# Projections of an attention block: granules of 512 instead of 256 moving columns, in four PSUM banks

## The chip, the core and the metric

The kernel runs on one core of a Trainium2 chip. The metric is the device time of one launch in microseconds (us). A core has a matrix engine (TensorE, PE in the profile, with its weight loads as PEld), a vector engine (VectorE, DVE), a scalar engine (ScalarE, ACT), GpSimd (POOL) and SyncE (SP), which here issues nearly all DMA transfers. Each engine works through its own queue in order and waits on semaphores for the others. TensorE multiplies a stationary 128x128 tile with moving columns and writes to PSUM, of which this kernel uses eight banks of 128 partitions x 512 float32.

## The reference

One decoder layer: RMSNorm of x (512 tokens, 1024 channels), one input projection whose columns are split among a state-space branch, an attention branch and gates, then two output projections, a gated sum, a last projection `w_o` and the residual. What matters here, cut:

```python
h = rms_norm(x, norm_w[layer])
proj = h @ w_in[layer]
u_s, z_s, q, k, v, z_a, r_s, r_a = jnp.split(proj, offsets, axis=-1)
y_s = s5_branch(u_s, ...)                       # diagonal state space, GELU, GLU
y_s = (y_s * silu(z_s)) @ w_ssm_out[layer]
q = apply_partial_rope(rms_norm(q.reshape(B, L, 3, 8, 64), q_norm_w), positions)
k = apply_partial_rope(rms_norm(k.reshape(B, L, 3, 8, 64), k_norm_w), positions)
y_a = dilated_attention(q, k, v.reshape(B, L, 3, 8, 64))   # 3 head groups, 8 heads of 64
y_a = (y_a * silu(z_a)) @ w_attn_out[layer]
m = sigmoid(r_s) * y_s + sigmoid(r_a) * y_a
x = x + m @ w_o[layer]
```

All arithmetic is float32.

## The kernel before, in words

**Matmuls in three parts.** To multiply float32 values at the faster rate of the type fp32r, each operand is split into a high and a low part (`split`, lines 90 to 97: ACT rounds to the high part, DVE or POOL subtracts). One product is then three matmuls, `mm3` (lines 107 to 110): high x high, high x low, low x high. The normed input is kept transposed and split as `hT_hi`, `hT_lo` (1024 channels in 8 slices of 128, 512 tokens).

**Weights** come in the order of a list, `plan`. Each entry is a tile of 128 x 1024 values, 512 KB: `cm_spec` takes 128 columns over all 8 slices of the contraction; `tok_spec` takes 256 columns in two tiles, each of 4 slices (a half of the contraction). `load_w` lets SP issue a DMA for every separate run of columns (line 166), then splits the tile on ACT (line 93, `w_hi`) and DVE (line 95, `w_lo`). `get_w` hands out the next tile and starts the loads two tiles ahead; three tiles of each part are in turn.

**Two kinds of projection.** `cm_unit` has the weights stationary and 512 tokens of `hT` moving: 8 x 3 matmuls of 512 moving columns into one bank `pj`. `tok_granule` has 128 tokens of `hT` stationary and 256 weight columns moving: for two tiles, four row blocks and four slices 96 matmuls of 256 moving columns, into two banks `pj`, each of which holds two row blocks. q, k and the v of head groups 1 and 2 are made by `tok_granule`; v of group 0 by `v0_unit`, which is a `cm_unit` and a transposition.

**Attention rounds.** Four rounds (`hp`) take two heads of each of the three groups. `qk_granule(hp, g)` projects q and k of a group (128 columns each), copies the banks (`qraw`, line 796), squares (798), sums per head (799), forms the reciprocal root with three Newton steps (lines 99 to 105, on 128x16 values), scales (807) and rotates on POOL (814 to 819); its `finish` transposes on TensorE (827) and splits into `QT`, `KA`, `KB` (835, 836). `scores` makes scores with mask, exponentials and weights in `Pt`; `values` transposes `Pt` and multiplies it with V, into the one bank of pool `ps_o`. The last round has the gate units `ra_unit` (each a `cm_unit`) beside it; two of the eight (`n_ra`) are done before the attention stage.

**PSUM.** Pool `ps_p` has 3 banks (`pj`, all projections), `ps_g` 4 banks (everything else: transposes, scores, the state-space branch), `ps_o` one.

**Order of the work.** The program names an engine for every instruction. The order within each engine's queue and the waits are made by a planner from its own cost estimates when the program is built (`schedule_with_timeline_sim=True`): where an instruction isn't ready by these estimates, a later one of the program goes first. So matmuls of the next projection stand between the pieces of `scores` and `values`, and the queues do not follow the program line by line.

**The end.** The last stage multiplies `mT_hi`, `mT_lo` (stationary) with `w_o` in four steps of 256 columns, each of the form of `tok_granule`; DVE adds the residual (line 1065) and SP stores (line 1066).

The rounds of the program before:

```python
    qk_round(0)()
    for hp in range(NP):
        Pt = scores(hp, *QK)
        if hp < NP - 1:
            fin = qk_round(hp + 1)       # three granules; each finish one granule later
            values(hp, Pt, V)
            V = new_v()
            finv = v0_unit(hp + 1, V)
            fin()
            v_granule(hp + 1, V)
            finv()
```

Of the kernel before, what the change touches and what calls it, by code (L numbers as in the profile page):

```python
# [52 lines left out]
def tile_hybrid_block(ctx: ExitStack, tc: tile.TileContext, x, positions, norm_w, w_in, lam_re, lam_im,  # L53
# [12 lines left out]
    ps_p = ctx.enter_context(tc.tile_pool(name="ps_p", bufs=3, space=PSUM))  # L66
    ps_g = ctx.enter_context(tc.tile_pool(name="ps_g", bufs=4, space=PSUM))
# [68 lines left out]
    for c in range(KT):  # L136
        plan.append(cm_spec(w_ssm_out, c * P))
    for hp in range(NP):
# [5 lines left out]
    for c in range(n_ra, KT):  # L144
# [3 lines left out]
    for c in range(4):  # L148
        plan += tok_spec(w_o, (c * 256, 256))
# [641 lines left out]
    def qk_granule(hp, g, QT, KA, KB):  # L791
        pss = tok_granule()
        raw = big.tile([P, NB, 256], F32, name="qraw", tag=("s7a", "s7b")[g % 2])
        sq = sml.tile([P, NB, 4], F32, name="ssq")
        for b in range(2):
            act.copy(raw[:, 2 * b:2 * b + 2].rearrange("p r c -> p (r c)"), pss[b])  # L796
            s = t2k("qsq")
            act.activation(s, pss[b], AF.Square)  # L798
            dve.tensor_reduce(sq[:, 2 * b:2 * b + 2], s.rearrange("p (r h d) -> p r h d", r=2, h=4), AX.X, ALU.add)  # L799
        v = sml.tile([P, NB * 4], F32, name="qv")  # L800
        rstd = sml.tile([P, NB * 4], F32, name="qrstd")
        qa = sml.tile([P, NB * 4], F32, name="qa")
        qb = sml.tile([P, NB * 4], F32, name="qb")
        dve.tensor_scalar(v, sq.rearrange("p r h -> p (r h)"), 1.0 / HD, EPS, op0=ALU.mult, op1=ALU.add)
        rsqrt(rstd, v, [P, NB * 4], qa, qb)
        rv = raw.rearrange("p r (h d) -> p (r h) d", h=4)
        dve.tensor_tensor(rv, rv, rstd.unsqueeze(2).broadcast_to([P, NB * 4, HD]), op=ALU.mult)  # L807

        t1 = sml.tile([P, NB * 2, 2, 16], F32, name="rt1", bufs=1)
        t2 = sml.tile([P, NB * 2, 2, 16], F32, name="rt2", bufs=1)  # L810
        rh = raw.rearrange("p r (a h d) -> p (r a) h d", a=2, h=2)
        cv = tC[:, g].rearrange("p r a d -> p (r a) d").unsqueeze(2)
        sv = tS[:, g].rearrange("p r a d -> p (r a) d").unsqueeze(2)
        pool.tensor_tensor(t1, rh[:, :, :, 0:16], cv.broadcast_to([P, NB * 2, 2, 16]), op=ALU.mult)  # L814
        pool.tensor_tensor(t2[:, :, :, 0:8], rh[:, :, :, 8:16],
                           sv[:, :, :, 0:8].broadcast_to([P, NB * 2, 2, 8]), op=ALU.mult)
        pool.tensor_tensor(t2[:, :, :, 8:16], rh[:, :, :, 0:8],
                           sv[:, :, :, 8:16].broadcast_to([P, NB * 2, 2, 8]), op=ALU.mult)
        pool.tensor_tensor(rh[:, :, :, 0:16], t1, t2, op=ALU.add)

        def finish():
            for a in range(2):
                ps = bank("qtp")
                pn = ps.rearrange("p (b r j) -> p r b j", r=4, b=4)
                for r in range(NB):
                    o = pn[:, r] if g == 0 else ps[:, r * P:(r + 1) * P]
                    pe.transpose(o, raw[:, r, a * P:(a + 1) * P], ident)  # L827
                if a == 0 or g == 0:
                    parts = [(slice(0, P), QT[0][:, g], QT[1][:, g]) if a == 0 else (slice(0, P), KA[0], KA[1])]
                else:  # L830
                    parts = [(slice(64 * h, 64 * h + 64), KB[0][64 * h:64 * h + 64, g - 1, h],
                              KB[1][64 * h:64 * h + 64, g - 1, h]) for h in range(2)]
                for sl, hi, lo in parts:
                    w = wcol[sl, g, a:a + 1]
                    act.activation(hi, ps[sl], AF.Copy, scale=w)  # L835
                    dve.scalar_tensor_tensor(lo, ps[sl], w, hi.bitcast(F32), op0=ALU.mult, op1=ALU.subtract)
        return finish
# [159 lines left out]
    def qk_round(hp):  # L997
        fin = None
        for g in range(NG):
            f = qk_granule(hp, g, *QK)  # L1000
            if fin:
                fin()
            fin = f
        return fin

    qk_round(0)()

    for hp in range(NP):
        Pt = scores(hp, *QK)
        if hp < NP - 1:  # L1010
            fin = qk_round(hp + 1)
            values(hp, Pt, V)
            V = new_v()
            finv = v0_unit(hp + 1, V)
            fin()
            v_granule(hp + 1, V)
            finv()
        else:
            for c in range(n_ra, KT - 2):
# [26 lines left out]
    for cc in range(4):  # L1046
        pss = [ps_p.tile([P, 512], F32, name="pj", tag="pj") for _ in range(2)]
        for kh in range(2):
            hi, lo = get_w()
            for b in range(2):  # L1050
                for rr in range(2):
                    r = 2 * b + rr
                    o = pss[b][:, rr * 256:(rr + 1) * 256]
                    for k in range(4):
                        kk = 4 * kh + k
                        mm3(o, mT_hi[:, kk, r * P:(r + 1) * P], mT_lo[:, kk, r * P:(r + 1) * P],
                            hi[:, k], lo[:, k], kh == 0 and k == 0 and rr == 0, kh == 1 and k == 3)
        cols = slice(cc * 256, (cc + 1) * 256)
        for b in range(2):
            ob = t2k("ob").rearrange("p (r c) -> p r c", r=2)  # L1060
            psb = pss[b].rearrange("p (r c) -> p r c", r=2)
            parts = [slice(0, 2)] if cc < 3 else [slice(0, 1), slice(1, 2)]
            for w in parts:
                rw = slice(2 * b + w.start, 2 * b + w.stop)
                dve.tensor_tensor(ob[:, w], psb[:, w], xr[:, rw, cols], op=ALU.add)
                sp.dma_start(ov[:, rw, cols], ob[:, w])
# [28 lines left out]
```

## Time and profile before

| | |
|---|---|
| median of 3 runs | 743.52 us (743.5 to 743.62) |
| profiled execution, its own time | 745.33 us |
| its span, first to last instruction | 743.5 us |
| mean granted clock of TensorE | 0.983 |
| busy: PE, DVE, ACT, POOL | 94%, 63%, 45%, 23% of the span |
| DMA | 85.51 MB moved, queue q1 busy 44.1% of 16 engines |

A matmul's row in the timeline is its start, its length, and its operands (written tile, moving operand, stationary operand). Matmuls are pipelined: the length runs on beside the next matmul, so what one occupies is the distance from its start to the next start. In a row of a group stand the count, the busy time, the mean length in ns, and behind the bar the idle time of the engine ahead of these instructions and what ended it. In a row of the stage windows stand the window, its length, the busy time and (in brackets) the instructions of PE, PEld, DVE, ACT and POOL, the granted clock, the DMA share and GB/s.

### The profile page before, as it was taken

How to read it: one execution, taken by the hardware profiler on the slowest of the kernel's cores; microseconds unless marked ns; L12 is line 12 of the kernel's file. 1: busy time of each engine (PE TensorE's matmuls, PEld its weight loads, DVE VectorE, ACT ScalarE, POOL GpSimd, SP SyncE). 2: the span in 40 equal slices, each digit the busy share in tenths (PEclk: the TensorE clock that was granted, in tenths of full speed). 3: DMA queues.
4: the chain of work that ended last, by engine and by line, in shares of the span. 5: the costliest groups of instructions: out<-in, count | busy, mean ns of one | idle time of the engine just before them, and what ended most of it. 6: DMA issues, size and time to landing. Idle time of an engine off the chain costs nothing.

```text
span 743.5 us, 13321 instructions
## 1 busy us (share of the span) xinstructions
PE 702.2 (94%) x5221; PEld 615.8 (83%) x5221; DVE 468.4 (63%) x958; ACT 336.7 (45%) x628; POOL 168.7 (23%) x304
## 2 busy tenths in 40 slices
PE   3699999999979688999999999999999999999998
PEld 2687788788857477888899999899999989778997
DVE  6768757989867454674336679667747654536631
ACT  6443544233388574433143475464446435433310
POOL 3345631110001001550001224142304311200000
PEclk9899999999999899999999999999999999999999
DMA  9754654674637765447324212213211321356321
GB/s 203 129 143 110 159 114 105 144 178 118 120 101 138 136 132 143 154 133 217 91 80 120 86 57 85 59 30 98 85 46 57 95 77 57 109 179 226 124 100 57
DMA packets 156014, 85.51 MB, mean 115 GB/s; under 512 B 40232, under 2 KB 148144, under 8 KB 155824
## 3 DMA queue, kind: packets, MB, share of 16 engines
q1 hardware_dynamic: 155936, 84.66, 44.1%
q8 instruction: 41, 0.67, 0.4%
q14 instruction: 21, 0.17, 0.1%
q10 hardware_dynamic: 16, 0.00, 0.0%
HBM read 73.18 MB, written 11.47 MB: 114 GB/s over the span
## 4 chain that ended last, share of the span: by engine, by line
PE 78%; DMA 8%; DVE 6%; SPq 3%; ACT 2%; issue 2%; POOL 0%; DVEq 0%; ACTq 0%
PE pj L110 21%; PE pj L109 21%; PE pj L108 21%; DMA w_raw<-in_w_in_dram 4%; PE ot L926 3%; PE ptp L940 2%; PE sps L870 2%; PE qtp L827 1%; DMA kd<-kt 1%; DVE w_lo L95 1%; PE xps L282 1%; DMA dd<-kd 1%; PE wps L271 1%; DMA gd<-th 1%; DVE scn L610 1%
## 5 line engine op out<-in xcount | busy, mean ns | idle before, releaser
L93 ACT ACTIVATE w_hi<-w_raw 128x1024 fp32r<-128x1024 f32 x100 | 105.9, 1060 | 200.6 <-PE pj L109 89.4
L95 DVE TENSOR_TENSOR w_lo<-w_raw,w_hi 128x1024 fp32r<-128x1024 f32 x98 | 124.2, 1268 | 64.1 <-ACT w_hi L93 62.9
L108 PE MATMUL pj<-hT_hi,w_hi 128*128 128x512 f32 (+1 forms) x344 | 135.0, 395 | 9.7 <-ACT w_hi L93 5.6
L109 PE MATMUL pj<-w_lo,hT_hi 128*128 128x256 f32 x512 | 144.0, 281 | 0.0
L110 PE MATMUL pj<-w_hi,hT_lo 128*128 128x256 f32 x512 | 143.9, 281 | 0.0
L108 PE MATMUL pj<-w_hi,hT_hi 128*128 128x256 f32 x512 | 143.8, 281 | 0.0
L109 PE MATMUL pj<-hT_lo,w_hi 128*128 128x512 f32 (+1 forms) x344 | 133.5, 389 | 0.4 <-DVE hT_lo L228 0.4
L110 PE MATMUL pj<-hT_hi,w_lo 128*128 128x512 f32 (+1 forms) x344 | 133.3, 388 | 0.1
L109 PEld LDWEIGHTS pj<-w_lo,hT_hi 128*128 128x128 f32 x512 | 96.2, 188 | 1.4 <-issue 0.7
L108 PEld LDWEIGHTS pj<-w_hi,hT_hi 128*128 128x128 f32 x512 | 96.0, 188 | 1.1 <-issue 0.9
L110 PEld LDWEIGHTS pj<-w_hi,hT_lo 128*128 128x128 f32 x512 | 96.0, 188 | 0.7
L108 PEld LDWEIGHTS pj<-hT_hi,w_hi 128*128 128x128 f32 x344 | 67.0, 196 | 23.1 <-ACT w_hi L93 5.8
L110 PEld LDWEIGHTS pj<-hT_hi,w_lo 128*128 128x128 f32 x344 | 66.5, 193 | 14.5 <-issue 0.8
L109 PEld LDWEIGHTS pj<-hT_lo,w_hi 128*128 128x128 f32 x344 | 66.8, 194 | 13.5 <-DVE hT_lo L228 0.8
L814 POOL TENSOR_TENSOR rt<-qraw,tC 128x256 f32<-128x256 f32 x12 | 16.5, 1371 | 127.0 <-DVE qraw L807 93.0
L109 PE MATMUL pj<-w_lo,mT_hi 128*128 128x256 f32 x128 | 36.2, 283 | 0.0
L110 PE MATMUL pj<-w_hi,mT_lo 128*128 128x256 f32 x128 | 36.2, 283 | 0.0
L108 PE MATMUL pj<-w_hi,mT_hi 128*128 128x256 f32 x128 | 36.2, 283 | 0.0
L849 ACT ACTIVATE Pt<-Pt,st 128x256 f32<-128x256 f32 (+1 forms) x64 | 31.0, 487 | 5.0 <-DVE st L847 4.8
L799 DVE TENSOR_REDUCE ssq<-qsq 128x8 f32<-128x512 f32 x24 | 16.4, 685 | 26.3 <-ACT qsq L798 26.2
L835 ACT ACTIVATE qkp<-qtp,wcol 128x512 fp32r<-128x512 f32 (+1 forms) x32 | 20.7, 685 | 20.7 <-PE qtp L827 15.6
L796 ACT COPY qraw<-pj 128x512 f32<-128x512 f32 x24 | 14.1, 586 | 35.0 <-PE pj L110 34.8
(272 smaller groups left out, 1368.5 us busy)
## 6 DMA issues: line engine op xcount, KB each, us to landing
w_raw<-in_w_in_dram SPq DMA_DIRECT2D x40, 512.0 KB
w_raw<-in_w_in_dram SPq DMA_DIRECT2D x64, 256.0 KB
dd<-kd SPq DMA_DIRECT2D x8, 512.0 KB
w_raw<-in_w_glu_dram SPq DMA_DIRECT2D x8, 512.0 KB
w_raw<-in_w_ssm_out_dram SPq DMA_DIRECT2D x8, 512.0 KB
w_raw<-in_w_o_dram SPq DMA_DIRECT2D x8, 512.0 KB
x_all<-in_x_dram SPq DMA_DIRECT2D x4, 512.0 KB
ud<-uT SPq DMA_DIRECT2D x8, 256.0 KB
```

Source lines behind the costliest of these rows:

```text
L93: act.activation(hi, src, AF.Copy, scale=scale)
L95: e.tensor_tensor(lo, src, hi.bitcast(F32), op=ALU.subtract)
L108: pe.matmul(o, lh, rh, start=first, stop=False, skip_group_check=True)
L109: pe.matmul(o, lh, rl, start=False, stop=False, skip_group_check=True)
L110: pe.matmul(o, ll, rh, start=False, stop=last, skip_group_check=True)
L799: dve.tensor_reduce(sq[:, 2 * b:2 * b + 2], s.rearrange("p (r h d) -> p r h d", r=2, h=4), AX.X, ALU.add)
L814: pool.tensor_tensor(t1, rh[:, :, :, 0:16], cv.broadcast_to([P, NB * 2, 2, 16]), op=ALU.mult)
L835: act.activation(hi, ps[sl], AF.Copy, scale=w)
L849: act.activation(o, o, AF.Exp, bias=nm, scale=-1.0, accum_out=st[:, kind, 1, h, b:b + 1])
L870: pe.matmul(pss[h][:, cols], QT[x_][po, 0, cb], KA[y_][po, ks], start=n == 0, stop=n == 2, skip_group_check=True)
L926: pe.matmul(o, v, pts[h][:, (2 * i + k) * P:(2 * i + k + 1) * P], start=first, stop=kind == 1 and b == NB - 1 and k == 1, skip_group_check ...
L940: pe.transpose(ps[:, (2 * i + k) * P:(2 * i + k + 1) * P], Pt[:, h, kind, 2 * bb + i, k * P:(k + 1) * P], ident)
```

## The change

Where two narrow granules followed each other, one wide granule takes their place: 512 moving weight columns in four banks, one for each row block, with the weights in four tiles that each hold a quarter of the contraction (2 of 8 slices).

- `wide_spec` and `wide_granule` are new. Round by round, q and k of groups 0 and 1 are one wide granule (`qk_first`); q and k of group 2 with v of groups 1 and 2 are the second (`qk_second`). In the first round, whose v is made earlier, group 2 stays narrow (`qk_third`).
- The norms of groups 0 and 1 go through one chain, on 128x32 values (`qk_norm`). Their transposes (`qk_turn`) stand ahead of the second quarter of the second granule in the program, `values` ahead of its third.
- A unit `ra_unit` moves from the last round into the first.
- `w_o` is done in two wide granules; each row block has one addition and one store.
- `ps_p` has 4 banks instead of 3, `ps_g` 3 instead of 4.

```diff
-    ps_p = ctx.enter_context(tc.tile_pool(name="ps_p", bufs=3, space=PSUM))
-    ps_g = ctx.enter_context(tc.tile_pool(name="ps_g", bufs=4, space=PSUM))
+    ps_p = ctx.enter_context(tc.tile_pool(name="ps_p", bufs=4, space=PSUM))
+    ps_g = ctx.enter_context(tc.tile_pool(name="ps_g", bufs=3, space=PSUM))
...
+    def wide_spec(w, *cols):
+        return [(section(w, 2 * h, 2 * h + 2, *cols), 2, 512) for h in range(4)]
...
     for hp in range(NP):
-        for g in range(NG):
-            plan += tok_spec(w_in, (Q0 + g * 512 + hp * P, P), (K0 + g * 512 + hp * P, P))
-        if hp > 0:
+        plan += wide_spec(w_in, head(Q0, 0, hp), head(K0, 0, hp), head(Q0, 1, hp), head(K0, 1, hp))
+        if hp == 0:
+            plan += tok_spec(w_in, head(Q0, 2, hp), head(K0, 2, hp))
+            plan.append(cm_spec(w_in, RA0 + n_ra * P))
+        else:
+            plan += wide_spec(w_in, head(Q0, 2, hp), head(K0, 2, hp), head(V0, 1, hp), head(V0, 2, hp))
             plan.append(cm_spec(w_in, V0 + hp * P))
-            plan += tok_spec(w_in, (V0 + 512 + hp * P, P), (V0 + 1024 + hp * P, P))
...
+    def wide_granule(th, tl, mid=None):
+        pss = [ps_p.tile([P, 512], F32, name="pj", tag="pj") for _ in range(NB)]
+        for kq in range(4):
+            if mid:
+                mid(kq)
+            hi, lo = get_w()
+            for r in range(NB):
+                for k in range(2):
+                    kk = 2 * kq + k
+                    mm3(pss[r], th[:, kk, r * P:(r + 1) * P], tl[:, kk, r * P:(r + 1) * P], hi[:, k], lo[:, k],
+                        kk == 0, kk == KT - 1)
+        return pss
...
+    def qk_first(mid=None):
+        pss = wide_granule(hT_hi, hT_lo, mid)
+        raws = [new_raw(0), new_raw(1)]
+        sq = sml.tile([P, NB, 8], F32, name="ssq")
+        for r in range(NB):
+            for i in range(2):
+                act.copy(raws[i][:, r], pss[r][:, 256 * i:256 * i + 256])
+            squares(sq[:, r], pss[r])
+        qk_norm((0, 1), raws, sq)
+        return raws
+
+    def qk_second(hp, mid=None):
+        pss = wide_granule(hT_hi, hT_lo, mid)
+        raw = new_raw(0)
+        V = new_v()
+        ...
+        for r in range(NB):
+            act.copy(raw[:, r], pss[r][:, 0:256])
+            squares(sq[:, r], pss[r][:, 0:256])
+            act.copy(V[:, 1:3, r], pss[r][:, 256:512].rearrange("p (g c) -> p g c", g=2))
+        qk_norm((2,), [raw], sq)
+        return raw, V
...
-    qk_round(0)()
+    raws = qk_first()
+    ...
+    raw = qk_third(turns)
+    ra_unit(n_ra)
+    qk_turn(2, raw, *QK)
 
     for hp in range(NP):
         Pt = scores(hp, *QK)
         if hp < NP - 1:
-            fin = qk_round(hp + 1)
-            values(hp, Pt, V)
-            V = new_v()
+            raws = qk_first()
+
+            def mid(kq):
+                if kq == 1:
+                    turns()
+                if kq == 2:
+                    values(hp, Pt, V)
+
+            raw, V_next = qk_second(hp + 1, mid)
+            V = V_next
             finv = v0_unit(hp + 1, V)
-            fin()
-            v_granule(hp + 1, V)
+            qk_turn(2, raw, *QK)
             finv()
...
-    for cc in range(4):
-        pss = [ps_p.tile([P, 512], F32, name="pj", tag="pj") for _ in range(2)]
-        ...
+    for cc in range(2):
+        pss = wide_granule(mT_hi, mT_lo)
+        cols = slice(cc * 512, (cc + 1) * 512)
+        for r in range(NB):
+            ob = t2k("ob")
+            dve.tensor_tensor(ob, pss[r], xr[:, r, cols], op=ALU.add)
+            sp.dma_start(ov[:, r, cols], ob)
```

More of the change, by code (lines that the diff above doesn't have):

```diff
@@ L147, in tile_hybrid_block @@
         plan.append((section(w_attn_out, 0, NP, (c * 256, 256)), NP, 256))
[L148 to L149 removed]
+    for c in range(2):
+        plan += wide_spec(w_o, (c * 512, 512))
     taken = [0]
@@ L794, in qk_granule @@
-        sq = sml.tile([P, NB, 4], F32, name="ssq")
+        mid()
+        raw = new_raw(0)
+        sq = sml.tile([P, NB, 8], F32, name="ssq")[:, :, 0:4]
         for b in range(2):
             act.copy(raw[:, 2 * b:2 * b + 2].rearrange("p r c -> p (r c)"), pss[b])
[L797 to L800, printed above, removed]
@@ L817, in qk_granule @@
[L817 to L836, printed above, removed]
```

107 lines of the change are left out of this document (60 added, 47 removed).

## The prediction

> **What bounds the kernel now.** I read the page first, then the stage windows, then TensorE's groups by shape, then its timeline, because a matmul's listed length overlaps the next one and only the distance between starts says what it occupies.
>
> ```profile
> span 743.5 us, 13321 instructions
> PE 702.2 (94%) x5221; PEld 615.8 (83%) x5221; DVE 468.4 (63%) x958; ACT 336.7 (45%) x628; POOL 168.7 (23%) x304
> PEclk9899999999999899999999999999999999999999
> PE 78%; DMA 8%; DVE 6%; SPq 3%; ACT 2%; issue 2%; POOL 0%; DVEq 0%; ACTq 0%
> ```
> ```profile
> 379.60:739.90 360.30, 360.30 (x2797) 334.66 (x2795) 212.56 (x538) 159.09 (x315) 72.76 (x180) 1.00 0.30 91
> ```
>
> The reader is to see that TensorE carries 78% of the chain that ends last, and that in the window which holds everything the change rewrites (first q/k granule to last output matmul) it is busy 360.30 of 360.30 us at full granted clock. DVE (212.56), ACT (159.09) and POOL (72.76) have room there, and DMA is at a 0.30 share. So in this stage time is the sum of TensorE's issue distances. I now take these from starts.
>
> ```profile
> L109 PE MATMUL pj<-w_lo,hT_hi 128*128 128x256 f32 x512 | 144.0, 281 | 0.0
> L108 PE MATMUL pj<-w_hi,mT_hi 128*128 128x256 f32 x128 | 36.2, 283 | 0.0
> L110 PE MATMUL pj<-hT_hi,w_lo 128*128 128x512 f32 x296 | 119.1, 402 | 0.0
> L110 PE MATMUL pj<-yT_hi,w_lo 128*128 128x512 f32 x64 | 24.7, 389 | 0.0
> ```
> ```profile
> 395.73 0.28 PE L110 MATMUL pj<-w_hi,hT_lo 128*128 128x256 f32 x1
> ...
> 403.50 0.28 PE L110 MATMUL pj<-w_hi,hT_lo 128*128 128x256 f32 x1
> ```
> ```profile
> 639.61 0.40 PE L110 MATMUL pj<-hT_hi,w_lo 128*128 128x512 f32 x1
> ...
> 649.88 0.40 PE L109 MATMUL pj<-hT_lo,w_hi 128*128 128x512 f32 x1
> ```
> ```profile
> 679.65 0.39 PE L109 MATMUL pj<-aT,w_hi 128*128 128x512 f32 x1
> ...
> 693.47 0.39 PE L110 MATMUL pj<-aT,w_lo 128*128 128x512 f32 x1
> 693.70 0.28 PE L108 MATMUL pj<-w_hi,mT_hi 128*128 128x256 f32 x1
> ...
> 739.65 0.28 PE L110 MATMUL pj<-w_hi,mT_lo 128*128 128x256 f32 x1
> ```
>
> Distances: 256 columns with hT stationary, 66 steps in 7.77 us = 117.7 ns; 256 columns with mT stationary, 383 steps in 45.95 us = 120.0 ns; 512 columns with hT moving, 44 steps in 10.27 us = 233.4 ns; 512 columns with aT moving, 61 steps in 13.82 us = 226.6 ns. Halving the number of matmuls thus saves little: two narrow ones cost 235.4 or 240.0 ns, one wide one 226.6 to 233.4.
>
> **The change part by part.**
>
> *The stream.* A token granule is 2 weight halves x 4 row blocks x 4 k x 3 = 96 narrow matmuls; a wide one is 4 x 4 x 2 x 3 = 96 wide ones and does the work of two. Rounds 0 to 3 hold 12 q/k granules and rounds 1 to 3 hold 3 v granules; all but round 0's third become wide: 14 narrow granules, 1344 matmuls, turn into 672. The output projection's 384 (three lines of 128) become 192. No row has hT or mT stationary with 512 moving columns, so I bound it by the two 512-column distances. With hT: 1344 x 117.7 = 158.2 us before; after, 672 x 233.4 = 156.8 (gain 1.4) or 672 x 226.6 = 152.3 (gain 5.9). With mT: 384 x 120.0 = 46.1 before; 192 x 233.4 = 44.8 (gain 1.3) or x 226.6 = 43.5 (gain 2.6). A loss is excluded only as far as 233.4 is the largest full-clock distance here. I take 233.4 where hT takes part, as in every 512-column hT unit, and 226.6 for mT, which has the tiles that yT had (389 ns listed, like aT's, against hT's 402). Sum: -4.0 us.
>
> The Trainium skill, "TensorE: Matmul & The Clock Gate", section "Back-to-back issue gap", gives a warm matmul its columns over 2.4 plus 2.5 ns: a fixed cost of only 2.5 ns. By it a pair falls from 218.4 to 215.8 ns and the whole stream gains 864 x 2.5 = 2.2 us (an estimate from that page). Its 109.2 and 215.8 ns lie below the measured 117.7 and 226.6, so the trace decides. The same section's 131 ns for a sustained 512-column stream is not what this trace shows, at 226.6.
>
> *Switches.* Leaving the projections for a float32 block and coming back costs extra:
>
> ```profile
> 443.76 0.38 PE L110 MATMUL pj<-w_hi,hT_lo 128*128 128x256 f32 x1
> 443.98 0.28 PE L108 MATMUL pj<-w_hi,hT_hi 128*128 128x256 f32 x1
> ...
> 445.04 0.28 PE L108 MATMUL pj<-w_hi,hT_hi 128*128 128x256 f32 x1
> 445.25 0.97 PE L870 MATMUL sps<-qkp 64*128 64x256 f32 x6
> ```
>
> The first matmul after scores takes 220 ns and the last before them 210, against 118: 0.2 us for each stretch of filler. Turning two head groups together makes 8 transpose blocks out of 12: -4 x 0.1 = -0.4 us. The general banks go from 4 to 3, so scores (pairs of banks) and values (pairs of ptp banks) must step aside more often. I take one more stretch in each of the 8 calls: +1.6 us; ends 0 and, at two or three more, +4.
>
> *Norm chain.* What is late next is the transposes, waiting for this chain:
>
> ```profile
> L796 ACT COPY qraw<-pj 128x512 f32<-128x512 f32 x24 | 14.1, 586 | 35.0 <-PE pj L110 34.8
> L798 ACT ACTIVATE qsq<-pj 128x512 f32<-128x512 f32 x24 | 14.5, 604 | 0.0
> L799 DVE TENSOR_REDUCE ssq<-qsq 128x8 f32<-128x512 f32 x24 | 16.4, 685 | 26.3 <-ACT qsq L798 26.2
> L104 DVE SCALAR_TENSOR_TENSOR qb<-qa,qv 128x16 f32<-128x16 f32 x36 | 6.7, 186 | 1.1
> L807 DVE TENSOR_TENSOR qraw<-qraw,qrstd 128x1024 f32<-128x1024 f32 x12 | 14.7, 1224 | 0.6
> L814 POOL TENSOR_TENSOR rt<-qraw,tC 128x256 f32<-128x256 f32 x12 | 16.5, 1371 | 127.0 <-DVE qraw L807 93.0
> L815 POOL TENSOR_TENSOR rt<-qraw,tS 128x128 f32<-128x128 f32 x12 | 5.5, 460 | 0.0
> L819 POOL TENSOR_TENSOR qraw<-rt,rt 128x256 f32<-128x256 f32 x12 | 9.9, 829 | 0.9
> ```
>
> For two groups: last bank's copies and square about 1.5 (an estimate; the 256-column copy has no row and lies below 586 ns), reduce 0.7, 12 small operations x 0.19 = 2.2, first scaling 1.2, then POOL 2 x (1.37 + 2 x 0.46 + 0.83) = 6.2: 12 us. It lies beside the second granule, 96 x 0.233 = 22 us, so it costs nothing; without that cover it would cost up to 12 us a round. The third group's chain is 1.5 + 0.7 + 2.2 + 1.2 + 3.1 = 9 us with only the v0 unit behind it in program order (24 x 0.233 = 5.6 us, where a v granule followed too). The other 3.4 us must come from the next round's granule or, in the last round, from ra units. Both exist, and the trace before shows TensorE filled at such places; I take 0, and +3.4 at the other end. One rsqrt chain fewer a round frees DVE, which waits elsewhere: 0.
>
> *Four banks at once.* ACT empties a bank in about 1.1 us (two short copies and a square, back to back) while the next bank's last 6 matmuls take 6 x 0.233 = 1.4 us, so the next granule finds its first bank free: 0. ACT gets 8 short copies for 4 long ones per first granule, at a 44% load: 0.
>
> *Weights.* A quarter feeds 24 x 0.233 = 5.6 us, a half fed 48 x 0.118 = 5.7.
>
> ```profile
> L93 ACT ACTIVATE w_hi<-w_raw 128x1024 fp32r<-128x1024 f32 x100 | 105.9, 1060 | 200.6 <-PE pj L109 89.4 <-PE pj L110 54.3 <-DMA w_raw<-in_w_in_dram 41.6
> 713.51 0.38 SPq L166 DMA_DIRECT2D w_raw<-in_w_o_dram  x1
> ```
>
> Splitting is unchanged (1.06 us on ACT a tile). SP issues 4 DMAs of 128 KB a q/k/v tile for 2 of 256 KB: 7 x 4 x 4 = 112 for 56, at about 0.38 us 1.5 us of each 5.6. Behind them on SP queue only later tiles, ra reloads and output stores: 0.
>
> *The end.*
>
> ```profile
> 739.97 0.76 DVE L1065 TENSOR_TENSOR ob<-pj,xr 128x256 f32<-128x256 f32 x2 [2.12 <-PE pj L110]
> 740.42 0.81 SPq L1066 DMA_DIRECT2D out_dram<-ob  x2
> ```
>
> Two additions and two stores follow the last matmul; afterwards one of each, the same bytes: one issue less, -0.4 us.
>
> *Ahead of the attention stage* only the pools change: pj banks 3 to 4, general banks 4 to 3. A wait that the fourth bank could end is this:
>
> ```profile
> 245.50 0.79 PE L108 MATMUL pj<-hT_hi,w_hi 128*128 128x512 f32 x1 [4.10 <-ACT th L469]
> 246.09 0.63 PE L109 MATMUL pj<-hT_lo,w_hi 128*128 128x512 f32 x1
> 246.52 0.63 PE L110 MATMUL pj<-hT_hi,w_lo 128*128 128x512 f32 x1
> ```
>
> 4.1 us of idle, then about 12 matmuls at 430 instead of 233 ns (2.4 us): at best -6.5. Against it, eight state-space units each pass kps, cps, yps and yT through the general banks; one bank copy of 0.6 us exposed, with its hand-over 0.8, at each: +6.4. The ends balance and nothing says which is nearer; I take 0.
>
> Sum: -4.0 - 0.4 + 1.6 - 0.4 = -3.2 us. The profiled execution took 745.33 us (span 743.5 and 1.8 around it) and becomes 742.1; the median of the unprofiled runs lies 1.8 lower, so 743.5 becomes 740.3.
>
> **The rivals.**
>
> *A, the wide stream with hT goes at 226.6 ns:* 4.5 us more gain, 735.8. For it: yT and aT do so. Against: hT, with 512 columns, does not in the rows above.
>
> *B, no change:* the columns cost the same however they are cut (235 ns with hT, 240 with mT), or scores and values break up at the +4 end. Then 743.5 within 1.5 us. For it: 2 x 117.7 and 233.4 are already within 1%.
>
> *C, slower: three general banks in the state-space stage (205 to 290 us).* There TensorE already waits, so nothing covers a later kps or yps; +6.4 gives 746.7. It decides from (3.2 + 1.5) / 8 = 0.6 us a unit.
>
> *D, faster: the fourth pj bank ends the wait at 245.50:* 740.3 - 6.5 = 733.8. Against it: ACT, which ended that wait, sits in its own queue behind a store and would still be late for the next copies.
>
> *E, slower: banks cycled by fours pause TensorE long enough to lose its clock*, as after 241 us: one pause of that kind costs 4.1 + 2.4 = 6.5 us and gives 746.8. Against: the 1.1 against 1.4 us above. The Trainium skill, same page, section "A second HAM failure mode: psum-queue depth-cycling", tells of such loss by pauses between groups; the trace shows it only behind the 4.1 us wait.
>
> **How the numbers follow.** Forecast 0.43, A 0.13, D 0.06, B 0.20, C 0.13, E 0.05. A measurement of this kernel tells 0.2%, 1.5 us, from no change. The forecast, A and D are faster: 0.62; B the same: 0.20; C and E slower: 0.18. The likeliest case alone spans 738 to 742 (interruptions 0 to +4 less the part B holds); the range takes in A, B, C and E, and ends just above D: 734.5 to 747.
>
> **What would show it.** In the profile of the changed kernel: wide matmuls with hT stationary 233 ns apart (A: 227; B: 235 or more), with mT 227; TensorE busy throughout from the first wide granule to the last output matmul, that window 3 us shorter than 360.3; transposes of groups 0 and 1 inside the second granule with no idle time ahead of them; the state-space stage ending at the same time. Wrong if the stage before 380 us ends more than 2 us earlier or later, if idle time appears ahead of the third group's transposes or at a granule's first matmul, or if scores and values fall into many more pieces.

## The result, and the profile after

The changed kernel takes 750.67 us (median of 4 runs, 748.84 to 751.63), the kernel before 743.51 beside it: a ratio of 1.0098, 95% interval 1.0075 to 1.0121. It is slower by 7 us, where 3 us less was forecast, and outside the forecast's range of 734.5 to 747.

The page of the kernel after: span, busy time, granted clock, and the chain that ended last.

```profile
span 749.3 us, 11705 instructions
PE 690.5 (92%) x4357; PEld 568.9 (76%) x4357; DVE 468.6 (63%) x914; ACT 339.1 (45%) x662; POOL 167.6 (22%) x304
PEclk9899999999989996999999999999999999999999
PE 74%; ACT 7%; DVE 6%; DMA 6%; SPq 4%; issue 2%; POOL 1%; ACTq 0%; DVEq 0%
```

TensorE is busy for 690.5 us against 702.2: the change did save work on the engine that bounds the kernel, 11.7 us of it. The span grew by 5.8 us all the same, so TensorE now stands idle for 58.8 us instead of 41.3, and ACT's share of the chain rose from 2% to 7%. The stage windows say where. First the kernel before, then the one after; the cuts are the last x unit's matmul (tile xps), the last instruction of DVE's scan (Xs), the first product of gT, the first of the attention stage and the last output matmul, each by its start.

```profile
0.00:116.90 116.90, 95.34 (x775) 80.89 (x776) 80.98 (x195) 57.16 (x91) 51.86 (x73) 0.96 0.64 143
116.90:204.90 88.00, 88.00 (x477) 71.32 (x472) 79.71 (x112) 30.87 (x51) 12.38 (x16) 1.00 0.59 133
204.90:292.50 87.60, 71.38 (x798) 56.84 (x797) 49.35 (x70) 62.15 (x139) 7.61 (x19) 0.92 0.61 125
292.50:379.60 87.10, 87.10 (x386) 72.08 (x385) 45.02 (x43) 27.43 (x35) 24.07 (x16) 1.00 0.50 151
```
```profile
0.00:125.10 125.10, 102.69 (x816) 86.27 (x816) 86.32 (x197) 59.16 (x93) 48.96 (x73) 0.97 0.60 138
125.10:214.90 89.80, 84.58 (x460) 68.38 (x456) 80.11 (x112) 31.55 (x52) 10.61 (x16) 1.00 0.58 135
214.90:302.00 87.10, 66.86 (x773) 54.03 (x774) 45.97 (x67) 59.91 (x134) 7.22 (x19) 0.87 0.53 115
302.00:389.00 87.00, 87.00 (x385) 72.05 (x384) 47.09 (x43) 28.16 (x37) 25.70 (x17) 1.00 0.50 151
389.00:745.30 356.30, 349.21 (x1933) 288.21 (x1932) 208.42 (x495) 160.32 (x349) 75.14 (x180) 1.00 0.30 91
```

Two things happened. The attention stage, which the change rewrites, became 4.0 us shorter (356.30 for 360.30), though TensorE is no longer busy throughout: 349.21 of it. And the attention stage starts 9.4 us late, at 389.0 for 379.6. Of the first four stages only the first is really longer, by 8.2 us, with 41 more instructions on PE, and the second by 1.8, with 5.2 us of idle time on PE in it where there was none. The 9.4 us were lost where no matmul was rewritten. Last product to end of span is 749.3 - 745.06 = 4.2 us for 3.85. Together: 9.4 - 4.0 + 0.4 = 5.8.

What the first stage took on is seen by counting the projection matmuls alone (windows of tile pj on PE: window, length, busy, count, clock, DMA share, GB/s), before, then after:

```profile
0.00:116.90 116.90, 70.96 (x339) 0.96 0.64 143
116.90:204.90 88.00, 84.85 (x405) 1.00 0.59 133
204.90:292.50 87.60, 43.85 (x170) 0.92 0.61 125
```
```profile
0.00:125.10 125.10, 79.09 (x379) 0.97 0.60 138
125.10:214.90 89.80, 81.44 (x389) 1.00 0.58 135
214.90:302.00 87.10, 37.05 (x145) 0.87 0.53 115
```

Forty projection matmuls that used to run beside or after the scan now stand between the w and x units that the scan waits for (339, now 379). The scan ends 10.0 us later, and behind it only 145 are left instead of 170 to lie beside the state-space units. What put the scan off is the order itself. The rows of ACT and PE ahead of the last two xps in the changed kernel:

```profile
118.94 1.14 ACT L280 COPY W<-wps 128x512 f32<-128x512 f32 x2
...
122.86 0.40 PE L108 MATMUL pj<-hT_hi,w_hi 128*128 128x512 f32 x1
123.18 2.13 PE L290 MATMUL xps<-Uj,W 128*64 128x64 f32 x64
```

W is copied by 120.08, with it the banks of wps and of the xps before are empty, and the load of Uj landed at 111.0. Still xps starts at 123.18, behind 18 projection matmuls; in the kernel before 3 stand there. So at this place TensorE waited neither for a bank nor for data: the queue held other work first.

Behind the scan TensorE waits, before (first fence) and after:

```profile
207.33 0.34 PE L733 MATMUL yps<-ab,uss 128*64 128x64 f32 x4 [2.10 <-ACT uss L721]
266.91 0.30 PE L731 MATMUL yps<-dd,uss 128*64 128x64 f32 x3 [1.55 <-DMA dd<-kd]
```
```profile
217.16 0.48 PE L741 MATMUL yps<-ab,uss 128*64 128x64 f32 x4 [7.48 <-ACT uss L729]
278.63 0.34 PE L739 MATMUL yps<-dd,uss 128*64 128x64 f32 x4 [4.23 <-DMA dd<-kd]
290.89 0.37 PE L739 MATMUL yps<-dd,uss 128*64 128x64 f32 x2 [7.38 <-DMA dd<-kd]
```

The 7.48 us begin at 209.68, where the projections run out: the scan's last instruction on DVE starts only at 214.86, and then ACT still copies the last part of its result. Before, projections lasted to the scan's end, and 2.10 us were left. That the two waits for dd come from the same lack of other work is read from the order. From the scan's end to the first gT product, the whole of the first wait counted in, the idle time of all rows is 25.5 us for 16.2. The one long wait there for a bank to come free, the 4.10 us at 245.50 that the prediction showed, has become 1.09 us.

The idle time inside the attention stage, 7.1 us, has this form in rounds 2 and 3. First the norm chain (ACT's last square of the first granule, DVE, POOL), then TensorE:

```profile
525.36 0.64 ACT L861 ACTIVATE qsq<-pj 128x512 f32<-128x512 f32 x1
...
530.54 2.05 DVE L967 TENSOR_SCALAR Pt<-Pt,sd 128x128 f32<-128x128 f32 x8
530.56 5.31 POOL L960 COPY sfb<-sd 32x2 f32<-32x2 f32 x16 [8.46 <-DVE sd L956]
538.78 2.36 DVE L828 TENSOR_TENSOR qraw<-qraw,qrstd 128x1024 f32<-128x1024 f32 x2
546.01 0.74 POOL L839 TENSOR_TENSOR qraw<-rt,rt 128x256 f32<-128x256 f32 x1
```
```profile
525.67 0.50 PE L110 MATMUL pj<-w_hi,hT_lo 128*128 128x512 f32 x1
...
546.39 0.39 PE L110 MATMUL pj<-w_hi,hT_lo 128*128 128x512 f32 x1
546.62 1.47 PE L847 MATMUL qtp<-ident,qraw 128*128 128x128 f32 x12
549.85 0.66 PE L847 MATMUL qtp<-ident,qraw 128*128 128x128 f32 x4 [1.76 <-DVE qkp L856]
...
551.54 1.33 PE L1004 MATMUL ptp<-ident,Pt 128*128 128x128 f32 x7 [0.49 <-DVE qkp L856]
...
558.80 1.97 PE L990 MATMUL ot<-ptb,V 128*64 128x128 f32 x32
561.24 0.50 PE L108 MATMUL pj<-hT_hi,w_hi 128*128 128x512 f32 x1 [0.47 <-ACT V L887]
```

The chain runs from 525.4 to 546.75, 21 us: the scaling of Pt on DVE and 16 copies on POOL, both the scores' own, and splits of weights on DVE stand between its steps. By then all of the second granule is used up (91 matmuls from 525.67 to 546.39). Transposes of two groups want four general banks and have three, so the last four wait 1.76 us for DVE. `values` stand behind them in the program; they run with no projection beside them, and the next unit waits 0.47 us for a `pj` bank that ACT can't empty, since `V` is still being read. That is 2.7 us a round.

### The profile page after: what moved, and what is told of

Its sections match the earlier page's. It is cut to its first block, busy times and chain, and to the rows that moved or that the text cites. A ratio compares the mean times of both kernels' runs of the same rounds, so it can differ in the third digit from the quotient of the medians.

```text
span 749.3 us, 11705 instructions
## 1 busy us (share of the span) xinstructions
PE 690.5 (92%) x4357; PEld 568.9 (76%) x4357; DVE 468.6 (63%) x914; ACT 339.1 (45%) x662; POOL 167.6 (22%) x304
## 4 chain that ended last, share of the span: by engine, by line
PE 74%; ACT 7%; DVE 6%; DMA 6%; SPq 4%; issue 2%; POOL 1%; ACTq 0%; DVEq 0%
PE pj L108 21%; PE pj L110 21%; PE pj L109 21%; PE ot L990 2%; ACT uss L728 2%; PE ptp L1004 2%; DVE w_lo L95 2%; DMA w_raw<-in_w_in_dram 1%; PE xps L290 1%; ACT w_hi L93 1%; DMA ral<-rad 1%; DMA kd<-kt 1%; DMA Uj<-ud 1%; PE sps L934 1%; DMA dd<-kd 1%
## 5 line engine op out<-in xcount | busy, mean ns | idle before, releaser
L109 PE MATMUL pj<-w_lo,hT_hi 128*128 128x512 f32 (+1 forms) x288 | 106.1, 368 | 0.0
L108 PE MATMUL pj<-w_hi,hT_hi 128*128 128x512 f32 (+1 forms) x288 | 105.7, 369 | 0.0
L110 PE MATMUL pj<-w_hi,hT_lo 128*128 128x512 f32 (+1 forms) x288 | 105.1, 368 | 0.0
L108 PEld LDWEIGHTS pj<-w_hi,hT_hi 128*128 128x128 f32 x288 | 54.1, 188 | 9.4 <-issue 0.2
L110 PEld LDWEIGHTS pj<-w_hi,hT_lo 128*128 128x128 f32 x288 | 54.1, 188 | 9.1
L109 PEld LDWEIGHTS pj<-w_lo,hT_hi 128*128 128x128 f32 x288 | 54.1, 188 | 8.7
L739 PE MATMUL yps<-dd,uss 128*64 128x64 f32 x256 | 21.4, 265 | 11.6 <-DMA dd<-kd 11.6
L856 DVE SCALAR_TENSOR_TENSOR qkp<-qtp,wcol,qkp 128x512 fp32r<-128x512 f32 (+1 forms) x32 | 23.0, 745 | 13.6 <-ACT qkp L855 13.6
L739 PEld LDWEIGHTS yps<-dd,uss 128*64 128x64 f32 x256 | 17.6, 175 | 14.3 <-issue 9.1
L741 PE MATMUL yps<-ab,uss 128*64 128x64 f32 x256 | 21.4, 264 | 7.5 <-ACT uss L729 7.5
```

Of the source, the lines that this page charges most:

```text
L108: pe.matmul(o, lh, rh, start=first, stop=False, skip_group_check=True)
L109: pe.matmul(o, lh, rl, start=False, stop=False, skip_group_check=True)
L110: pe.matmul(o, ll, rh, start=False, stop=last, skip_group_check=True)
L739: pe.matmul(o[h], Uj[:, g, :], M[:, g, 64 * h:64 * h + 64], start=True, stop=False, skip_group_check=True)
L741: pe.matmul(o[h], Ss[:, g, :], ca[:, g, 4 * h:4 * h + 4, :], start=False, stop=True, skip_group_check=True)
```

## The experiments

TensorE's stages in each kernel, by the same marks as above (us; "idle" adds up the idle time of PE behind the first product of the attention stage; with a change of pools just ahead of that product, in e6_phase, e7, e9, e11, e12 and e15, 0.9 us of idle time stand in front of it):

| kernel | last xps | scan's end | attention starts | its length | idle in it | end of span |
|---|---|---|---|---|---|---|
| before | 116.9 | 204.9 | 379.6 | 360.1 | 0.0 | 743.5 |
| changed | 125.1 | 214.9 | 389.0 | 356.0 | 7.1 | 749.3 |
| e1_pools43 | 128.4 | 218.5 | 392.7 | 361.8 | 0.0 | 758.4 |
| e2_pools33 | 125.6 | 213.9 | 384.0 | 359.9 | 0.0 | 747.9 |
| e3_wide34 | 118.1 | 205.9 | 378.9 | 361.4 | 8.1 | 744.5 |
| e5_wo | 116.3 | 204.3 | 380.1 | 357.2 | 0.0 | 741.5 |
| e6_phase | 116.8 | 204.3 | 380.1 | 357.2 | 7.7 | 741.5 |
| e14_late | 116.9 | 205.6 | 378.6 | 357.1 | 7.7 | 739.8 |
| e15_early | 121.1 | 213.4 | 385.7 | 356.4 | 7.5 | 746.3 |
| e7_values0 | 117.5 | 205.1 | 378.1 | 354.5 | 4.3 | 736.8 |
| e11_xr | 117.1 | 204.4 | 377.5 | 355.2 | 6.0 | 737.0 |
| e12_v0xr | 116.3 | 203.2 | 379.0 | 352.8 | 2.9 | 736.2 |
| e9_ra | 117.5 | 204.4 | 381.0 | 359.9 | 9.4 | 745.0 |
| e16_best | 116.7 | 205.2 | 380.6 | 354.3 | 2.9 | 739.3 |

Each row is one profiled run. How far such rows can be compared is told by TensorE's order ahead of the attention stage (2425 instructions, by operation and tile): it is one and the same in the kernel before, e3, e5, e6, e7, e9, e11 and e12, whatever their attention code, and there the attention stage starts between 377.5 and 381.0 us. It is also the same in the changed kernel and e1, with 389.0 and 392.7. So some 2 us to either side in these columns are spread from run to run.

### The banks alone, in the kernel before

```diff
 # e1_pools43                                  # e2_pools33: ps_p stays at 3
-    ps_p = ...(name="ps_p", bufs=3, ...)
-    ps_g = ...(name="ps_g", bufs=4, ...)
+    ps_p = ...(name="ps_p", bufs=4, ...)
+    ps_g = ...(name="ps_g", bufs=3, ...)
```

> The kernel before with nothing changed but the two pools: pj banks 3 to 4, general banks 4 to 3. In the changed kernel the attention stage starts at 389.05 us instead of 379.59 (+9.5) while its window is 3.9 us shorter. Theory P (the pools cost the 9.5 us, because the state-space chain starts later): attention stage starts near 389, time near 753. Rival R (the rewritten attention code makes the planner order the early stage otherwise): starts at 379.6, time 743.5 within 1.5.

> The kernel before with 3 general banks instead of 4 and still 3 pj banks (one bank unused). Theory P1 (the missing general bank delays wps, xps and so the scan): attention stage starts near 389, time near 753, as with both edits. Theory P2 (the fourth pj bank lets more projection matmuls in ahead of the state-space units): starts near 379.6, time 743.5 within 1.5.

e1_pools43: 756.32 us, ratio 1.0145 (1.0122 to 1.0168), attention from 392.7 us. e2_pools33: 749.73 us, ratio 1.0073 (1.005 to 1.0097), attention from 384.0. The two numbers of the pools alone cost more than the whole change lost; theory P holds, and rival R falls. (The profiled run of e1 is the slowest of its five, 3.8 us above their median; by the medians e1 costs 11.9 us and e2 5.3.) Neither half carries it by itself: a general bank less costs 4.4 us ahead of the attention stage, and the fourth `pj` bank, which is one more and takes nothing from anyone in e1 that e2 hadn't taken already, costs as much again or more. Of e2's theories neither gives the time. P1 has the place right, the last xps is as late as with both edits (125.6 us). But 379 projection matmuls stand ahead of it too, so the general bank alone brings the forty forward; with the fourth `pj` bank 24 more move from behind the scan to beside it (365 and 169 in e2's next two windows). A further bank can make no instruction wait for a bank; it acts through the order that the planner makes with it. The windows of tile pj show that order in e1, the same three counts as in the changed kernel (389 and 145 in the next two):

```profile
0.00:128.40 128.40, 82.10 (x379) 0.96 0.59 134
```

### The new granules with the old pools, and w_o alone

```diff
 # e3_wide34: the changed kernel with ps_p 3, ps_g 4, and in wide_granule
-        pss = [ps_p.tile([P, 512], F32, name="pj", tag="pj") for _ in range(NB)]
+        pss = [ps_p.tile([P, 512], F32, name="pj", tag="pj") for _ in range(3)] + [bank("pj")]
 # e5_wo: the kernel before with wide_spec and this wide_granule for w_o only
```

> The changed kernel with the pools of before (3 pj, 4 general); a wide granule takes three pj banks and one general bank. Theory P: the early stage is that of before (attention starts near 379.6), the attention window keeps the 3.9 us, time 743.5 - 3.9 = 739.6 (738.5 to 741). Rival R: attention starts near 389 and the time stays near 750.

> The kernel before with the output projection alone in two wide granules (three pj banks and one general bank), pools as before. By the prediction's term: 384 matmuls at 120.0 ns become 192 at 226.6, -2.6 us, and one store issue less, -0.4: 740.5. If wide matmuls with mT went at 233.4: 741.8. If something hidden ended the stage (stores, weights): 743.5.

e3_wide34: 747.64 us, ratio 1.0037 (1.0012 to 1.0062), against the 739.6 expected. The stage ahead is back (378.9), but the attention stage has 361.4 us: what the wide matmuls save, idle time takes. Some of it, from the timeline of PE (first scores, which have no projection beside them; then the first matmul behind a weight tile that is late, once a round):

```profile
435.63 0.61 PE L108 MATMUL sps<-qkp 128*128 128x256 f32 x3 [0.75 <-ACT qkp L855]
...
446.20 0.50 PE L108 MATMUL pj<-w_hi,hT_hi 128*128 128x512 f32 x1 [0.31 <-ACT w_hi L93]
```

One granule fills all three `pj` banks and a general one, so the next can't begin before it is emptied; that this is why the scores stand bare was read from the order and not tried by itself. The new granules and the old pools don't go together. e5_wo: 742.31 us, ratio 0.9968 (0.995 to 0.9986), with the output stage (693.70 to 740.10 before, 694.00 to 737.70 in e5) at

```profile
693.70:740.10 46.40, 46.23 (x385) 46.02 (x383) 14.80 (x19) 7.13 (x8) 0.00 (x0) 1.00 0.28 91
```
```profile
694.00:737.70 43.70, 43.68 (x193) 35.85 (x191) 14.42 (x17) 7.14 (x8) 0.00 (x0) 1.00 0.26 88
```

2.7 us less for half the matmuls, as the stream term had it.

### Each stage with its own banks

```diff
 # e6_phase: the changed kernel; pools opened anew for the attention stage
-    ps_p = ...(name="ps_p", bufs=4, ...)
-    ps_g = ...(name="ps_g", bufs=3, ...)
+    open_pools(3, 4)          # closes ps_p and ps_g if open, opens them with these sizes
...
+    open_pools(4, 3)          # ahead of the first qk_first()
 # e14_late:  (3, 4), then (4, 3) already behind the last x unit
 # e15_early: (4, 3), then (3, 4) behind the last x unit, (4, 3) ahead of qk_first()
```

> The changed kernel in every line, except that the PSUM banks are dealt out twice: three projection and four general banks (as in the kernel before) up to the attention stage, then four and three (as in the changed kernel). Theory P (the loss is the bank split ahead of the attention stage, and is added to a gain of the attention stage that is there): first hT product of the attention stage at 379 to 380 us instead of 389.0, the stage itself still about 356 us against 360.1 before, so 751 - 9.5 = about 741 us, ratio to the kernel before 0.996 to 0.998. Rival N (the two do not add: attention was only shorter because it started late, its stores and weights being ahead): the stage grows back to 360 us and the time is 744 to 746, ratio 1.000 to 1.003.

> The changed kernel with three projection and four general banks up to the last x unit (xps, 117 us), and four and three from there to the end; the kernel with the two splits changes over at 380 us instead. Theory W (the loss is made among the w and x units, 60 to 125 us: in the changed kernel 379 projection matmuls stand ahead of the last xps, in the kernel before 339, so the scan begins and ends 10 us later and 24 projection matmuls fewer are left for the time behind it): last xps at 117 us, scan's end at 204 to 206, attention stage from 379 to 382 us, time within 2 us of the kernel with the two splits (743.4). Rival C of the prediction (the three general banks hold up the state-space stage, 205 to 290 us): scan's end at 204 to 206 too, but the last yT at 296 or later instead of 289 and attention from 386 us on, time 6 us or more above the kernel with the two splits.

> The mirror image: four projection and three general banks up to the last x unit, three and four from there to 380 us, then four and three. Theory W: last xps at 124 to 129 us, scan's end at 213 to 219, attention stage from 387 to 393 us, time 8 to 12 us above the kernel with the two splits. Rival C: scan's end within 3 us of the kernel before's 204.9, attention from 383 us at most, time within 3 us of the kernel with the two splits.

e6_phase: 743.36 us, ratio 0.9976 (0.9952 to 1.0001). Attention starts at 380.1 and keeps its 357.2 us: the loss ahead and the gain inside add, as theory P says. The time itself came out 2 us above the 741 expected, on a chip where the kernel before took 744.34; by it alone the gain is not shown, since the interval reaches 1.0001. e14_late: 741.77, ratio 0.9952 (0.9926 to 0.9977), attention from 378.6. The state-space stage does as well with three general banks as with four, so rival C's place is refuted. e15_early: 748.08, ratio 1.006 (1.0033 to 1.0086), attention from 385.7: four and three up to 121 us alone give 5.6 us of the loss, the scan ending 9.1 us later than in e6_phase. That is theory W in kind, but its 8 to 12 us is missed by half, and the last xps comes at 121.1 us where 124 to 129 were expected. More projection matmuls stand ahead of it here (e15_early, then e14_late):

```profile
0.00:121.10 121.10, 75.80 (x359) 0.97 0.61 138
```
```profile
0.00:116.90 116.90, 68.74 (x336) 0.97 0.63 143
```

336 and 339 matmuls leave the stage in time. 359 (e15) and 379 (e2) both put the scan off by 9 us and cost 5.6 and 4.4 us, with 169 matmuls left behind the scan. The changed kernel and e1, with 379 ahead and 145 left, lose 9.4 and 13.1. So two parts show in the counts: projections ahead of the scan's inputs, and fewer of them left behind the scan. What the two halves of the program cost does not add up to 9.4 (5.6 and -1.5, each within some 2 us); why the planner leaves fewer behind the scan only with four and three banks throughout was not tried.

### Where values stand, and a load ahead of its queue

```diff
 # e7_values0 = e6_phase and          # e11_xr = e6_phase and                # e12_v0xr = both
+    if kq == 0:                       -    sp.dma_start(xr, x[0]...)
+        values(hp, Pt, V)             +    pool.dma_start(xr, x[0]...)
     if kq == 1:
         turns()
-    if kq == 2:
-        values(hp, Pt, V)
```

> As the kernel with the two bank splits, and values of the round are emitted in the first quarter of the second granule, ahead of the transposes of groups 0 and 1, instead of in the third quarter behind them. Theory S (the 7.1 us of TensorE idle in the attention stage come from values standing in program order behind transposes that wait for the norm chain of 14.6 us): values run among projection matmuls, the V copies no longer wait for them (0.47 a round), the waits at the qtp and ptp banks (1.76 and 0.49 a round) shrink; idle in the stage falls to 1 to 3 us and the time by 4 to 6 us against the kernel with the two splits. Rival G (three general banks are what scores, values and the transposes of q and k wait for, wherever values stand): idle stays near 7 us, and the time is within 1 us of the kernel with the two splits. Rival F (values need filler that the first quarter does not have, and the scores behind them lose theirs): idle moves to the scores' start, as in the run where wide granules held a general bank, time 0 to 3 us longer.

> As the kernel with the two splits, with the load of xr issued from POOL's queue, and values left in the third quarter: the queue theory by itself. Theory X: TensorE's wait for DVE's ral in front of the aT products, 1.70 us in the kernel with the two splits, is gone, the other idle of its attention stage (6.9 of 8.6 us) stays, time 1 to 2 us less (741.5 to 742.5). Rival Y (the gain seen with values in the first quarter was spread from run to run): the wait stays, or the time is within 0.5 us of the kernel with the two splits.

> As the kernel with values in the first quarter, and the load of the residual x (xr, 128x4096) is issued from POOL's queue instead of SP's. In the changed kernel it stands on SP at 680.73 us ahead of the eight ral loads and waits there for the last read of Pt; the ral loads go out from 681.1 on, against 666.59 before, and DVE waits 6.64 us for them. Theory X (that queue holds up the merge of the r_a gate at the end): ral loads go out 10 us or more earlier, the TensorE wait of 1.09 us for DVE's ral in front of the aT products is gone and the end stage is 1 to 2.5 us shorter than in the kernel with values in the first quarter. Rival Y (the ral tiles come free no earlier, or the last aT is what that stage waits for): within 0.5 us of it.

The groups of PE in the attention stage with idle time, in e6_phase and then e12_v0xr (count, busy, mean ns, idle and what ended it):

```profile
L117 PE MATMUL pj<-hT_hi,w_hi 128*128 128x512 f32 x72 | 28.9, 401 | 1.4 <-ACT V L896 1.4
L1013 PE MATMUL ptp<-ident,Pt 128*128 128x128 f32 x120 | 18.5, 288 | 1.1 <-DVE qkp L865 1.0
L856 PE MATMUL qtp<-ident,qraw 128*128 128x128 f32 x96 | 12.9, 274 | 3.5 <-DVE qkp L865 3.5
L117 PE MATMUL pj<-aT,w_hi 128*128 128x512 f32 x32 | 12.2, 397 | 1.7 <-DVE ral L1119 1.7
```
```profile
L117 PE MATMUL pj<-hT_hi,w_hi 128*128 128x512 f32 x72 | 28.7, 398 | 0.9 <-ACT V L896 0.9
L999 PE MATMUL ot<-ptb,V 128*64 128x128 f32 x240 | 19.4, 280 | 1.8 <-DVE ptb L1020 1.8
...
L856 PE MATMUL qtp<-ident,qraw 128*128 128x128 f32 x96 | 13.7, 277 | 0.0
L117 PE MATMUL pj<-aT,w_hi 128*128 128x512 f32 x32 | 12.1, 394 | 0.0
```

e7_values0: 740.56 us, ratio 0.9947 (0.9926 to 0.9968), 2.8 us less than e6_phase where 4 to 6 were expected. Theory S holds in kind: the waits at qtp, 3.5 us, and behind them at ptp, 1.0, are gone with the same three general banks, so rival G falls. Idle time fell to 4.3 us where 1 to 3 were expected: the last round's values now wait 1.8 us for DVE, which they did not in e6_phase (why was not tried), V's copies still wait in two rounds, and the wait for ral stays. e11_xr: 741.76 us, ratio 0.996 (0.9934 to 0.9986); e12_v0xr: 739.18, ratio 0.9928 (0.9902 to 0.9954). Either way the wait of 1.7 us for DVE's ral is gone. By the time alone the step is not shown, since the intervals overlap; the queue shows it. SP in the changed kernel, then in e11_xr:

```profile
680.73 0.34 SPq L1113 DMA_DIRECT2D xr<-in_x_dram  x1
681.12 0.90 SPq L1104 DMA_DIRECT2D ral<-rad  x2
```
```profile
663.97 0.89 SPq L1114 DMA_DIRECT2D ral<-rad  x2
```

The load of xr waits for the buffer that Pt holds, and the ral loads stood behind it. Counted from the start of the attention stage they now go out at 286.5 us instead of 292.1.

### The r_a unit back in the last round

```diff
 # e9_ra = e6_phase and
-    ra_unit(n_ra)                                   # first round
...
-            for c in range(n_ra + 1, KT - 2):
+            for c in range(n_ra, KT - 2):           # last round
```

> As the kernel with the two bank splits, and the r_a unit that the change moved to the first round (filler for the third group's norm chain there) is put back into the last round, which has six of them again. Theory L (the last round, with five units, has too little work beside the last scores and values, and its tail of r_a store, r_a load and merge is late for it): the time falls by 1 to 2.7 us (the idle in front of the aT products, 1.09 us, and up to six waits of 0.3 us behind it), while the first round shows an idle of up to 9 us less what the scheduler finds. Rival M (the unit is needed where the change put it): time 2 to 6 us longer, with the idle in front of the third group's transposes in the first round.

e9_ra: 745.48 us, ratio 1.0009 (0.9979 to 1.0039), attention stage 359.9 us with 9.4 idle. Theory L falls: the unit is worth about 2.7 us of the stage where the change put it (357.2 against 359.9). The time itself, 2.1 us more, lies within the intervals. New idle time shows not ahead of the third group's transposes, as rival M had it, but in the first call of values, 2.1 us in four waits, where the projections are used up (the first of them):

```profile
468.78 0.55 PE L1012 MATMUL ptp<-ident,Pt 128*128 128x128 f32 x3 [0.52 <-DVE qkp L864]
```

### All three steps together

e16_best has e14_late's pools, values in the first quarter and xr on POOL's queue.

> Three steps together: three projection and four general banks up to the last x unit and four and three from there on, values in the first quarter of the second granule, xr from POOL's queue. Theory (the three causes are separate and add): attention stage from 378 to 380 us (as in the kernel with the later change-over), 353 us long as in the kernel with values first and xr on POOL, idle in it 3.8 us, time 737 to 739.5 us, ratio to the kernel before 0.990 to 0.994. Rival (the order behind the change-over is another one and gives part of it back): ratio 0.995 or more.

737.82 us (734.91 to 741.05), ratio 0.9897 (0.9874 to 0.992): the fastest of all, 1.0% ahead of the kernel before; the time lies within the 737 to 739.5 expected, the ratio just below its 0.990. The profiled run is the slowest of its six, so its 739.3 in the table is high; its attention stage starts at 380.6 us for the 378 to 380 expected and takes 354.3 for 353, with 2.9 us idle in it, as in e12_v0xr.

## Why the prediction was wrong, step by step

**The step that failed** is the last one, "Ahead of the attention stage only the pools change ... The ends balance and nothing says which is nearer; I take 0". It measured +9.4 us, beyond the upper end of +6.4. Both ends were built from waits for a bank in the state-space stage, the lower one read from the trace of before, the upper one estimated. The runs put the cause elsewhere: the planner, given another number of banks, brought forty projection matmuls forward to a place ahead of the scan's inputs (one general bank fewer is enough for that, e2), left fewer behind, and 9 us of waiting at the scan's end and behind it lost their cover. Rival C named the right line of the diff, with the wrong place (e14_late) and mechanism. Rival D's wait did shrink, from 4.10 to 1.09 us, and other waits took more than that back. Of rival E, a lost clock from cycling banks by fours, the attention stage shows nothing: its window has 1.00. In the stage behind the scan the prediction had the lower clock "only behind the 4.1 us wait"; in the trace of before it is 0.50 from 213.2 to 216.6 and from 261.0 to 264.4 us as well, behind waits of 2.33 and 3.45 us. The sign of the prediction that it gave for being wrong, the stage before 380 us ending over 2 us later, is the one that fired.

**The norm chain** is the second: forecast at 12 us beside 22 us of granule, cost 0. Its own steps were sized well (POOL's share 6.6 us, DVE's scaling 2.36), but they run on engines that are also doing the scores: 21 us. The transposes still came without idle time ahead of them; the cost fell on what stood behind them. With the V copies it is 5.9 of the 7.1 us idle. The term for four banks at once, 0, missed that the second granule's banks also wait for V, 0.47 us a round.

**The stream** was right in kind and too small. With mT stationary 191 steps from 701.77 to 745.06 us are 226.7 ns, the value taken:

```profile
701.77 0.39 PE L108 MATMUL pj<-w_hi,mT_hi 128*128 128x512 f32 x1
...
745.06 0.39 PE L110 MATMUL pj<-w_hi,mT_lo 128*128 128x512 f32 x1
```

With hT stationary 90 steps from 525.67 to 546.39 us are 230.2 ns, between 226.6 and 233.4: with 672 matmuls 2.1 us more gain than forecast, so rival A came half true. Counting every matmul from its start to the next start, less idle time, all hT-stationary ones fell from 173.1 to 167.0 us and the mT ones from 46.0 to 43.3: 8.8 against the 4.0 forecast, the rest being entries into and exits from filler. By the traces two narrow matmuls cost 2 x 117.7 - 230.2 = 5.2 ns more than a wide one with hT and 2 x 120.0 - 226.7 = 13.3 with mT. The 2.5 ns of fixed cost from the Trainium skill ("TensorE: Matmul & The Clock Gate", "Back-to-back issue gap") would have made 2.2 us of the gain, an estimate from that figure; the traces do not agree with it.

**Switches** had the wrong sign: +1.2 forecast. Between projections and other work TensorE changes over 74 times in the attention stage instead of 94, and scores cost 19.4 us for 23.4, values and their transposes together 1 us more. By itself the smaller general pool costs about what was taken for it at most, 1.6 us: the attention stage of e1 is 1.7 us longer than before, that of e2 0.1 shorter. Why scores are cheaper was not tried: e3, with 48 changes, has them at 23.4.

**Luck in the stage's sum.** The attention stage came out 4.0 us shorter, where the terms for it added up to 2.8. That is near by luck: 8.8 us from the stream for 4.0, and 4.0 from cheaper scores that nobody forecast, against 7.1 us of idle time where none was forecast.

**The rest.** The third group's chain cost 0, as taken; without the r_a unit 2.1 us of idle time came up in the first `values` (e9_ra). Weights in quarters cost 0: no wait for a load of them in the stage. But on SP the prediction named "only later tiles, ra reloads and output stores" behind the new DMAs and did not ask what held the reloads up: xr, 1.1 us. The end gained no 0.4 us and lost as much.

## What to carry to other kernels

Where a planner writes the order, a pool's size is an input to that order for the whole program, also where nothing was rewritten: compare, stage by stage, how many filler instructions stand ahead of the unit on which a long chain hangs, look whether that unit's inputs were ready before it started, and give each stage its own pools if they want different ones. Work that covers a wait is spent once: a chain that is hidden by using up the whole granule beside it leaves the next thing in program order bare, so ask what stands behind it and put independent work ahead. A chain of short steps on shared engines grows by the other work that stands between its steps, here from 12 to 21 us.

## What had not been expected of the hardware

With hT as the stationary operand 512 columns took 230.2 ns, with the weights stationary and hT moving 233.4 in the trace before: with mT stationary it was 226.7. So the distance between matmuls with 512 moving columns differed with the operands, all at a granted clock of 1.00; why was not tried. And with more idle time in it, the stage behind the scan was granted a lower clock, 0.87 for 0.92 in the stage windows above.
